# One-hots made earlier, a pair's gather moved between two parts of a down product, and other banks for the further rows' sums, in the expert layer of a two-layer encoder trunk

## The chip, the core and the metric

The kernel is one program on one core of a Trainium2 chip. The metric is the time of the whole program on the device in microseconds (us). The engines are named as the profile names them: PE is the matmul engine (PEld its weight loads), DVE the vector engine, ACT the scalar engine, POOL and SP the two others; SP issues nearly all loads. A PSUM bank is one of eight 128 x 512 float32 buffers into which PE writes.

## The reference, cut to what matters

256 rows of 1024 columns pass an even layer (mixers and a dense SwiGLU), an odd layer's banded attention, and then the expert layer, where the change is:

```python
def moe_swiglu(h, w_router, we_gate, we_up, we_down):
    t = h.reshape(b * s, d)                       # 256 x 1024
    logits = (t @ w_router).astype(F32)
    top_val, top_idx = lax.top_k(logits, TOP_K)   # 2 of 8 experts for each row
    gates = jax.nn.softmax(top_val, axis=-1)
    combine = jnp.einsum('tk,tke->te', gates, jax.nn.one_hot(top_idx, N_EXPERTS, dtype=F32))
    y = jnp.zeros_like(t)
    for e in range(N_EXPERTS):
        y = y + combine[:, e:e + 1] * ((silu(t @ we_gate[e]) * (t @ we_up[e])) @ we_down[e])
    return y
...
x = x + moe_swiglu(rms_norm(x, od_ffn_norm), ...)
```

The three weight tables of an expert are 1024 x 3584, 1024 x 3584 and 3584 x 1024 in float32: 352 MB for eight experts, read once.

## The kernel before

The expert layer begins at about 465 us of the span and lasts to its end. An expert computes only the rows that chose it. Their places (`pos`) are counted once; up to 64 of them are its *main* rows, up to 32 more its *further* rows ("over" in the code). A **one-hot** tile (`hot`, `hots`, through `one_hot` in line 910, on DVE) has a 1 where a row of the 256 goes to a place. The **gather** multiplies x with the one-hots on PE, so that an expert's rows stand turned in a tile `xg` (for even experts it lies in a tile that the trace calls oTh, for odd ones in xg); the products land in banks and DVE copies them out (line 935). One gather serves the two experts of a pair (2 and 3, 4 and 5, 6 and 7); experts 0 and 1 have one each.

The 3584 inner columns of an expert are cut into chunks of 512 to 2048 columns, and the loop at the end of `experts` goes over 18 chunks in a written order, the two experts of a pair one after the other by chunks, with the odd one's last chunk behind the even one's. For chunk i it runs the gate product (`cols`, ACT's Silu behind it), the up product (`cols`, DVE multiplies behind it), and then the down product of the chunk *before*, `down(i - 1, i)`. Each product comes in parts of up to four loaded weight tiles: main products of a part, then, under `arm`, the further rows' products of the same tiles. `arm` is a branch that every engine takes or passes by itself, on whether the expert has more than 64 rows. In this data the trace has products of the further rows for experts 1, 3, 5 and 7 and none for 0, 2, 4 and 6.

The down sums of an expert stand in two banks of its own for all its chunks: `y` (za in the trace) for the main rows, `yo` (zb) for the further ones. Behind an expert's last down part, its sums go back to the 256 rows: `split` (and `split_over` for the further rows) copies the bank as two float32r parts, ACT the high one and DVE the rest; products with the turned one-hot (`main_sums`, `over_sums`) bring them to row order, and DVE adds them, times the gate, to the total `yx` (`add_to`, line 1065). `turn` makes the turned one-hot dT of an expert when its last up product is done: one-hot on DVE, four products with an identity on PE, a copy on ACT. `turn_over` does this for the further rows one chunk later.

All other products (gate, up, transposes, gather, sums) write four banks in a fixed rotation: `banks(n)` hands out the next n and moves on, `banks(n, False)` only looks. They are named mm and tr in the trace.

What sets the order: within the expert layer PE, ACT and DVE each run their instructions in the order in which the code issues them (`in_order`). Loads go to SP's queue in the code's order (`feed.more` asks for as many tiles as were taken); a load waits there until its tile is free, that is, until PE has read what was in it.

Of the kernel before, what the change touches and what calls it, by code (L numbers as in the profile page):

```python
# [22 lines left out]
T = S // P  # L23
KB = D // P
# [23 lines left out]
def kernel(ctx: ExitStack, tc: tile.TileContext, A: dict, out: bass.AP):  # L48
# [9 lines left out]
    def mm(o, lhsT, rhs, start, stop):  # L58
        nc.tensor.matmul(o, lhsT, rhs, start=start, stop=stop, skip_group_check=True)  # L59
# [151 lines left out]
    x = consts.tile([P, T, D], F32, name="x")  # L211
# [610 lines left out]
    def starts(i):  # L822

        q = chunks[i + 1] if i + 1 < len(chunks) else None
        if not q or q.i or (q.e % 2 and q.e > 1):
            return []
        return [q.e] if q.e == 1 else [q.e, q.e + 1]
# [54 lines left out]
    with ExitStack() as ph:  # L882
# [31 lines left out]
        def hot(e):  # L914
            return one_hot(act.tile([P, T, CAP], F32, name="disp"), e, sel)

        def hots(es):

            o = act.tile([P, T, 2, CAP], F32, name="dispx")
            for j, e in enumerate(es):  # L920
                one_hot(o[:, :, j], e, selx)
            return o

        def gather(es, dx, kbs):

            m = len(es)
            nb = 4 // m
            for k in range(kbs[0], kbs[-1] + 1, nb):
                o = banks(1)[0][:, 0:4 * P].rearrange("p (b s) -> p b s", b=nb)
                for b in range(nb):  # L930
                    for t in range(T):
                        mm(o[:, b, 0:m * CAP].rearrange("p (e s) -> p e s", e=m), x[:, t, (k + b) * P:(k + b + 1) * P],
                           dx[:, t, 0:m], t == 0, t == T - 1)
                for j, e in enumerate(es):
                    nc.vector.tensor_tensor(rooms[e % 2][:, k:k + nb], o[:, :, j * CAP:(j + 1) * CAP],
                                            cst[:, C_GF1 + k:C_GF1 + k + nb, None].to_broadcast([P, nb, CAP]), op=OP.mult)
# [97 lines left out]
        class Expert:  # L1034
# [11 lines left out]

            def turn(self):
                self.dT = total[2][:, self.e % 2]
                self.dt = self.dt or hot(self.e)
                pt = banks(1)[0][:, 0:T * P].rearrange("p (t s) -> p t s", t=T)  # L1050
                self.turned(pt, MAIN, slice(0, MAIN))
                nc.scalar.activation(self.dT, pt, AF.Copy)
# [42 lines left out]

            def add_over(self, yy):
                self.split_over(yy)
                os = [banks(2) for _ in range(T)]
                self.over_sums(os, yy, True)
                for t in range(T):  # L1100
                    for h in range(2):
                        self.add_to(t, h, os[t][h])
# [41 lines left out]
        def banks(n, use=True):  # L1144
            found = [spin[(at[0] + i) % len(spin)] for i in range(n)]
            at[0] += n * use
            return found
# [9 lines left out]
        def experts(dt, feed, first, rvs):  # L1157


            found = [Expert(e, rvs[e] if rvs else None) for e in range(NE)]  # L1160
            found[0].dt, late = dt, []
            ao, turned, ready = aos, [], []

            def turn_main(i):
                n = chunks[i].n // 2
                turn(turned.pop()[:, 0:n], n, aTs[0][i % 2])

            def turn_over(i):
                n = chunks[i].n
                (turn_128 if by_128(n) else turn)(ao, over_width(n), aTs[1][i % 2])  # L1170

            def down(i, turns=None):
                q = chunks[i]
                x, cuts = found[q.e], spans(q.n // 256)
                for p, (i0, m) in enumerate(cuts):
                    dn = feed.take(m)
                    final = q.last and p == len(cuts) - 1
                    main_down(x.y, aTs[0][i % 2], i0, dn, q.n, q.i == 0, q.last)

                    def over():  # L1180
                        over_down(x.yo, aTs[1][i % 2], i0, dn, q.n, q.i == 0, q.last)

                    if turns and not p:
                        turn_main(turns)
                    if final and i == len(chunks) - 1:
                        x.finish(over)
                        return
                    if final:
                        x.split()
                        yy = act.tile([P, 2, 512], F32R, name="a")[:, :, 0:256]  # L1190
                    same = turns and not p and chunks[turns].e == q.e
                    with arm(x.rv):
                        over()
                        if same:
                            turn_over(turns)
                        if final:
                            x.add_over(yy)
                    if turns and not p and not same:
                        with arm(found[chunks[turns].e].rv):
                            turn_over(turns)  # L1200
                    feed.more(m)
                if q.last:
                    ready.append(x)

            def cols(x, main, over, n, mid=None, end=None):

                cuts = spans(KB // max(1, 2048 // n))
                nk = max(1, 2048 // n)
                for p, (i0, m) in enumerate(cuts):
                    tiles = feed.take(m)  # L1210
                    main_cols(main, x.xg, tiles, n, i0 * nk)
                    if mid and not p:
                        mid[0]()
                        with arm(mid[1]):
                            mid[2]()
                    if p == len(cuts) - 1:
                        end[0]()
                    with arm(x.rv):
                        over_cols(over, x.xg, tiles, n, i0 * nk)
                        if p == len(cuts) - 1:  # L1220
                            end[1]()
                    feed.more(m)

            for i, q in enumerate(chunks):
                x, n = found[q.e], q.n
                done = first and not i
                before = ready.pop() if ready else None
                m = len(parts(n))
                ow = over_width(n)
                part = ao[:, 0:ow]  # L1230

                def gate():
                    turned.insert(0, act.tile([P, 1024], F32, name="a"))
                    activate(turned[0], g, n)

                if done:
                    turned.append(act.tile([P, 1024], F32, name="a"))
                else:
                    g = banks(m)
                    go = banks(1)[0]  # L1240
                    mid = (lambda: turn_main(0), found[0].rv, lambda: turn_over(0)) if i == 1 else None
                    cols(x, g, go, n, mid, (gate, lambda: nc.scalar.activation(part, go[:, 0:ow], AF.Silu)))
                if late:
                    late.pop().turn_over()
                if before:
                    before.add(0)
                es = starts(i)
                if es:
                    dx = hots(es)

                def up():
                    a = turned[0]
                    if done:
                        g = banks(1)
                        first(g[0], 0)
                        nc.scalar.activation(a[:, 0:n // 2], g[0][:, 0:n // 2], AF.Copy)
                    activate(a, u, n, True)

                def up_over():
                    if done:  # L1260
                        go = banks(1)[0]
                        first(go, 1)
                        nc.scalar.activation(part, go[:, 0:ow], AF.Copy)
                    nc.vector.tensor_tensor(part, uo[:, 0:ow], part, op=OP.mult)

                u = banks(m)
                uo = banks(1)[0]
                cols(x, u, uo, n, None, (up, up_over))
                if es:
                    gather(es, dx, range(KB))  # L1270
                if before:
                    before.add(1)
                if q.last:
                    if not total:
                        total.extend(sums())
                    x.turn()
                    late.append(x)
                if i:
                    down(i - 1, i)
            late.pop().turn_over()  # L1280
            down(len(chunks) - 1)

# [107 lines left out]
        dx = hots([0])  # L1390
# [102 lines left out]
```

## Time and profile before

| | |
|---|---|
| time, median of 3 runs | 1319.26 us (1319.10 to 1319.53) |
| the profiled execution | 1318.28 us, of which its span is 1316.4 us |
| PE busy | 1269.1 us, 96% of the span |
| DVE busy, ACT busy | 380.1 us (29%), 322.0 us (24%) |
| PE's granted clock | 0.998 of full speed |
| bytes from HBM | 423.89 MB |

The span runs from the first to the last instruction; the profiled execution lies 1.9 us above its span and 1.0 us below the median. A view of instructions in order of time gives start, duration, engine, line, operation, out<-in by the program's names, the shape, the count, and in brackets how long the engine stood idle before and what released it. Idle times under 0.15 us are not shown in brackets. "PEq L1133" or "DVEq L1133" is the branch of `arm` as PE's or DVE's sequencer executes it. A product in float32 leaves two records (a transpose one), so counts in the trace are twice those of the program's order.

### The profile page before, as it was taken

The numbers are of one execution on the slowest core, as the hardware profiler recorded it, in microseconds if no ns is written. First come the engines' busy times: TensorE is split into PE (matmuls) and PEld (weight loads), VectorE is DVE, ScalarE is ACT, GpSimd is POOL, SyncE is SP. The second block draws the span as 40 slices with busy tenths as digits, with TensorE's granted clock in tenths as the row PEclk, the third lists the DMA queues.
The fourth block names the chain that finished last, engine by engine and source line by source line (L and its number), as shares of the span: only waits on it lengthen the run. The fifth ranks groups of instructions, "written<-read, shape, count | busy, mean of one in ns | idle before, by whom it ended". The sixth has DMA issues, their size and how long they took to land. (4 is left out here: it accounts for less than half of the span.)

```text
span 1316.4 us, 19363 instructions
## 1 busy us (share of the span) xinstructions
PE 1269.1 (96%) x7791; PEld 695.5 (53%) x7791; DVE 380.1 (29%) x735; ACT 322.0 (24%) x593; POOL 11.1 (1%) x38
## 2 busy tenths in 40 slices
PE   9999999999999989999999999999999999999996
PEld 6777888888777744343444333444333344333443
DVE  7965554446788510000111000111100001110001
ACT  7665544446566400100000000000000000000000
POOL 0000000000000000000000000000000000000000
PEclk9999999999999999999999999999999999999999
DMA  9623555555454989999899999999999999999980
GB/s 348 234 68 127 190 172 181 192 192 182 162 156 147 397 313 410 421 422 420 327 420 422 420 422 424 399 411 419 424 421 421 422 388 420 423 422 421 417 350 36
DMA packets 90245, 426.60 MB, mean 324 GB/s; under 512 B 7568, under 2 KB 10256, under 8 KB 59408
## 3 DMA queue, kind: packets, MB, share of 16 engines
q1 hardware_dynamic: 88768, 422.28, 80.4%
q0 software_dynamic: 640, 2.10, 0.7%
q8 instruction: 82, 1.34, 0.4%
q10 hardware_dynamic: 720, 0.60, 0.1%
q14 instruction: 35, 0.29, 0.1%
HBM read 423.89 MB, written 1.05 MB: 323 GB/s over the span
## 5 line engine op out<-in xcount | busy, mean ns | idle before, releaser
L59 PE MATMUL mm<-w,hTh 128*128 128x512 f32 x736 | 240.1, 400 | 0.9 <-DVE w L143 0.6
L143 DVE TENSOR_TENSOR w<-raw,w 128x1024 fp32r<-128x1024 f32 (+1 forms) x127 | 153.7, 1213 | 90.7 <-ACT w L142 90.2
L59 PEld LDWEIGHTS mm<-w,hTh 128*128 128x128 f32 x736 | 137.8, 188 | 33.3 <-DVE w L143 1.5
L142 ACT ACTIVATE w<-raw 128x1024 fp32r<-128x1024 f32 (+1 forms) x127 | 133.5, 1052 | 86.5 <-PE mm L59 51.3
L59 PE MATMUL mm<-w,hTl 128*128 128x512 f32 x368 | 146.5, 398 | 0.0
L1153 DVE TENSOR_TENSOR a<-tr,a 128x512 f32<-128x512 f32 (+1 forms) x16 | 10.0, 625 | 258.0 <-PE tr L59 151.9
L59 PE MATMUL za<-raw,hTh 128*64 128x512 f32 x360 | 81.5, 595 | 0.5 <-PEq L1133 0.4
L59 PEld LDWEIGHTS mm<-w,hTl 128*128 128x128 f32 x368 | 69.4, 188 | 14.8
L1153 DVE TENSOR_TENSOR a<-mm,a 128x512 f32<-128x512 f32 (+1 forms) x16 | 10.0, 624 | 222.7 <-PE mm L59 141.6
L59 PE MATMUL tr<-raw,xg 128*64 128x512 f32 (+4 forms) x400 | 63.8, 541 | 1.0 <-issue 0.4
L59 PE MATMUL tr<-rawb,xg 128*64 128x512 f32 (+4 forms) x504 | 59.6, 456 | 1.8 <-DVEq L1133 1.5
L59 PE MATMUL za<-rawb,hTh 128*64 128x512 f32 x256 | 57.6, 593 | 0.4 <-PEq L1133 0.4
L59 PE MATMUL mm<-w,oTh 128*64 128x512 f32 (+2 forms) x212 | 54.8, 517 | 2.4 <-DVEq L1133 1.5
L59 PE MATMUL mm<-raw,oTh 128*64 128x512 f32 (+1 forms) x232 | 47.2, 532 | 4.9 <-DVEq L1133 2.5
L59 PE MATMUL za<-w,hTh 128*64 128x512 f32 x224 | 50.5, 595 | 0.4 <-PEq L1133 0.4
L59 PEld LDWEIGHTS za<-raw,hTh 128*64 128x64 f32 x360 | 26.3, 137 | 46.0 <-issue 43.4
L59 PE MATMUL tr<-w,xg 128*64 128x512 f32 (+4 forms) x304 | 48.4, 530 | 0.3 <-PEq L1133 0.3
L59 PE MATMUL mm<-raw,xg 128*64 128x512 f32 (+4 forms) x320 | 48.3, 539 | 0.3 <-DMA rawb<-in_od_we_down 0.3
L255 DVE TENSOR_TENSOR oTl<-za,oTl 128x512 fp32r<-128x512 f32 x8 | 5.5, 690 | 138.5 <-ACT oTl L254 70.9
L59 PE MATMUL mm<-rawb,oTh 128*64 128x512 f32 (+1 forms) x204 | 42.9, 557 | 1.8 <-ACTq L1133 1.2
L981 ACT ACTIVATE hTh<-mm 128x512 f32<-128x512 f32 (+1 forms) x17 | 8.6, 544 | 141.3 <-PE mm L980 123.1
L59 PEld LDWEIGHTS tr<-rawb,xg 128*32 128x32 f32 (+1 forms) x504 | 24.0, 122 | 35.1 <-issue 29.2
(340 smaller groups left out, 1488.6 us busy)
## 6 DMA issues: line engine op xcount, KB each, us to landing
raw<-in_od_we_down SPq DMA_DIRECT2D x45, 1024.0 KB, 16.5
rawb<-in_od_we_down SPq DMA_DIRECT2D x32, 1024.0 KB, 18.4
raw<-in_od_we_gate SPq DMA_DIRECT2D x29, 1024.0 KB, 16.6
raw<-in_od_we_up SPq DMA_DIRECT2D x28, 1024.0 KB, 18.9
w<-in_od_we_down SPq DMA_DIRECT2D x28, 1024.0 KB, 16.8
rawb<-in_od_we_up SPq DMA_DIRECT2D x27, 1024.0 KB, 19.4
rawb<-in_od_we_gate SPq DMA_DIRECT2D x23, 1024.0 KB, 17.7
w<-in_od_we_gate SPq DMA_DIRECT2D x20, 1024.0 KB, 15.5
```

Source lines behind the costliest of these rows:

```text
L59: nc.tensor.matmul(o, lhsT, rhs, start=start, stop=stop, skip_group_check=True)
L142: nc.scalar.activation(hi[:, s], r[:, s], AF.Copy)
L143: nc.vector.tensor_tensor(lo[:, s], r[:, s], hi[:, s].bitcast(F32), op=OP.subtract)
L255: nc.vector.tensor_tensor(lo, src, hi.bitcast(F32), op=OP.subtract)
L981: nc.scalar.activation(dst[:, b:b + n], pt[:, 0:n], AF.Copy)
L1153: nc.vector.tensor_tensor(a[:, c:c + w], o[:, 0:w], a[:, c:c + w], op=OP.mult)
```

## The change

Three edits, and nothing else in the program:

1. The one-hot that `turn` needs is made for every expert's last chunk right behind the gate product (and the addition of t = 0 of an expert just finished), ahead of the up product, instead of in `turn`, behind the up product.
2. The gather for a new expert or pair is no longer issued behind the up product of chunk i and ahead of `turn`; it is handed to `down(i - 1, i, rows)` and issued behind that product's first part, with its transposes and further rows.
3. `add_over`, the further rows' sums, no longer takes four banks of the rotation. The sums of rows 0 to 127 (t = 0) go to the expert's own down banks `y` and `yo`; those of rows 128 to 255 go to the third and the fourth of the next four banks, without moving the rotation.

```diff
             def turn(self):
                 self.dT = total[2][:, self.e % 2]
-                self.dt = self.dt or hot(self.e)
...
             def add_over(self, yy):
                 self.split_over(yy)
-                os = [banks(2) for _ in range(T)]
+                os = [[self.y, self.yo], banks(4, False)[2:]]
                 self.over_sums(os, yy, True)
...
-            def down(i, turns=None):
+            def down(i, turns=None, rows=None):
...
                     feed.more(m)
+                    if rows and not p:
+                        gather(*rows, range(KB))
...
+                if q.last and not x.dt:
+                    x.dt = hot(q.e)
                 es = starts(i)
-                if es:
-                    dx = hots(es)
+                rows = (es, hots(es)) if es else None
...
                 cols(x, u, uo, n, None, (up, up_over))
-                if es:
-                    gather(es, dx, range(KB))
...
-                    down(i - 1, i)
+                    down(i - 1, i, rows)
```

**PE, around the first pair's gather**, behind the up product of expert 1's last chunk (in the names, dispx is the pair's one-hot and x the rows; disp is the one-hot of `turn`; za<-raw,hTh and za<-w,hTh are the first down part of expert 0; a and aos are what is transposed). Before:

```order
L59 MATMUL mm<-raw,xg 32x512 x8
L1133 UNCONDITIONAL_BRANCH x2
L59 MATMUL mm<-dispx,x 128x192 x4
L59 MATMUL tr<-dispx,x 128x192 x8
L59 MATMUL mm<-dispx,x 128x192 x4
L59 MATMUL mm<-ident,disp 64x128 x4
L59 MATMUL za<-raw,hTh 64x512 x8
L59 MATMUL za<-w,hTh 64x512 x8
```

After, from the first product behind the same branch:

```order
L59 MATMUL mm<-ident,disp 64x128 x4
L59 MATMUL za<-raw,hTh 64x512 x8
L59 MATMUL za<-w,hTh 64x512 x8
L980 MATMUL tr<-ident,a 128x128 x8
L1132 COMPARE_AND_BRANCH
L59 MATMUL zb<-raw,oTh 32x256 x16
L59 MATMUL zb<-w,oTh 32x256 x16
L1132 UNCONDITIONAL_BRANCH x2
L1132 COMPARE_AND_BRANCH
L980 MATMUL mm<-ident,aos 128x128 x4
L1132 UNCONDITIONAL_BRANCH x2
L59 MATMUL mm<-dispx,x 128x192 x4
```

The turned one-hot and the first down part now stand ahead of the gather, and the gather stands behind the transposes of expert 1's last chunk.

**DVE, at the same place** (line 910 is the one-hot, line 935 the gather's copies, L1153 and L1264 the multiplications behind the up product). Before:

```order
L1133 COMPARE_AND_BRANCH
L1264 TENSOR_TENSOR aos<-mm,aos 128x512
L1133 UNCONDITIONAL_BRANCH x2
L935 TENSOR_TENSOR oTh<-mm,cst 128x192
L935 TENSOR_TENSOR xg<-mm,cst 128x192
L935 TENSOR_TENSOR oTh<-tr,cst 128x192
L935 TENSOR_TENSOR xg<-tr,cst 128x192
L935 TENSOR_TENSOR oTh<-tr,cst 128x192
L935 TENSOR_TENSOR xg<-tr,cst 128x192
L935 TENSOR_TENSOR oTh<-mm,cst 128x192
L935 TENSOR_TENSOR xg<-mm,cst 128x192
L910 TENSOR_SCALAR disp<-slots,pos,sel 128x96 x2
```

After:

```order
L910 TENSOR_SCALAR disp<-slots,pos,sel 128x96 x2
L910 TENSOR_SCALAR dispx<-slots,pos,selx 128x96 x4
L1132 COMPARE_AND_BRANCH
L1132 UNCONDITIONAL_BRANCH x2
L1152 TENSOR_TENSOR a<-tr,a 128x512 x2
```

The one-hot of `turn` stood behind the gather's eight copies and now stands ahead of the multiplications behind the up product.

**DVE, at the end of expert 0's down product** (bank numbers kept; L255 are the parts of `split` and `split_over`, L1065 is `add_to`; the gate product that follows on PE begins in bank mm_3961, in both versions). Before:

```order
L255 TENSOR_TENSOR oTl_4778<-za_3962,oTl_4778 128x512
L1133 COMPARE_AND_BRANCH
L255 TENSOR_TENSOR a_5196<-zb_3964,a_5196 128x256
L1065 SCALAR_TENSOR_TENSOR yx_4775<-mm_3961,comb_3640,yx_4775 128x512
L1065 SCALAR_TENSOR_TENSOR yx_4775<-tr_3910,comb_3640,yx_4775 128x512
L1065 SCALAR_TENSOR_TENSOR yx_4775<-tr_3911,comb_3640,yx_4775 128x512
L1065 SCALAR_TENSOR_TENSOR yx_4775<-mm_3960,comb_3640,yx_4775 128x512
L1133 UNCONDITIONAL_BRANCH x2
```

After:

```order
L255 TENSOR_TENSOR oTl_4778<-za_3962,oTl_4778 128x512
L1132 COMPARE_AND_BRANCH
L255 TENSOR_TENSOR a_5196<-zb_3964,a_5196 128x256
L1064 SCALAR_TENSOR_TENSOR yx_4775<-za_3962,comb_3640,yx_4775 128x512
L1064 SCALAR_TENSOR_TENSOR yx_4775<-zb_3964,comb_3640,yx_4775 128x512
L1064 SCALAR_TENSOR_TENSOR yx_4775<-tr_3911,comb_3640,yx_4775 128x512
L1064 SCALAR_TENSOR_TENSOR yx_4775<-mm_3960,comb_3640,yx_4775 128x512
L1132 UNCONDITIONAL_BRANCH x2
```

Banks mm_3961 and tr_3910, in which the next gate product begins, are no longer read inside the branch.

## Rows read from the trace of the kernel before

**Rows 1.** Busy time by stretch: engines, PE's clock, DMA's share, GB/s

```profile
core 0: us, PE busy (x) PEld busy (x) DVE busy (x) ACT busy (x) POOL busy (x), PEclk, DMA share, GB/s
700.00:780.00 80.00, 76.86 (x488) 30.93 (x488) 9.80 (x19) 5.22 (x12) 0.00 (x0) 1.00 1.01 423
1280.00:1300.00 20.00, 18.26 (x218) 9.49 (x218) 4.01 (x8) 0.77 (x2) 0.00 (x0) 1.00 0.01 3
```

**Rows 2.** PE's waits: for whom, us in total, times, longest

```profile
PE tr L59 <- DVE disp L910: 5.5, 4, 1.7
PE mm L59 <- DVEq L1133: 4.0, 3, 1.5
PE mm L59 <- DVE disp L910: 3.3, 3, 1.4
PE tr L59 <- DVEq L1133: 3.0, 2, 1.5
...
PE mm L59 <- DMA rawb<-in_od_we_down: 0.7, 2, 0.4
```

**Rows 3.** Loads into tiles w, issued from 1176 to 1179 us

```profile
L838 SPq DMA_DIRECT2D w<-in_od_we_up x3: 327/328/423, 1176.7 to 1177.7; - x3
...
DMA to landing us min/median/max: 13.2/15.1/17.3
```

**Rows 4.** PE in order of time: the product that reads these tiles

```profile
1203.42 3.65 PE L59 MATMUL mm<-w,oTh 128*64 128x512 f32 x16
```

**Rows 5.** PE in order of time: products with one-hots of experts 0, 1, 2, 7

```profile
562.14 3.63 PE L59 MATMUL mm<-rawb,oTh 128*64 128x512 f32 x16
565.92 0.66 PE L59 MATMUL tr<-ident,disp 128*64 128x128 f32 x8
...
626.58 1.57 PE L59 MATMUL mm<-dispx,x 128*128 128x192 f32 x8
...
632.99 0.68 PE L59 MATMUL mm<-ident,disp 128*64 128x128 f32 x8 [0.95 <-DVE disp L910]
...
778.02 0.66 PE L59 MATMUL mm<-ident,disp 128*64 128x128 f32 x8 [1.43 <-DVE disp L910]
...
1287.88 0.68 PE L59 MATMUL tr<-ident,disp 128*64 128x128 f32 x8 [1.74 <-DVE disp L910]
```

**Rows 6.** PE in order of time: gate products behind a passed branch

```profile
470.73 0.65 PE L59 MATMUL mm<-raw,oTh 128*64 128x512 f32 x2 [0.93 <-DVEq L1133]
...
651.29 1.08 PE L59 MATMUL mm<-raw,oTh 128*64 128x512 f32 x4 [1.52 <-DVEq L1133]
...
747.55 0.65 PE L59 MATMUL tr<-rawb,oTh 128*64 128x512 f32 x2 [0.30 <-PEq L1133]
```

**Rows 7.** ACT and DVE in order of time, 649 to 652 us

```profile
649.81 0.60 ACT L254 ACTIVATE oTl<-za 128x512 fp32r<-128x512 f32 x1 [6.38 <-PE za L59]
...
650.44 0.69 DVE L255 TENSOR_TENSOR oTl<-za,oTl 128x512 fp32r<-128x512 f32 x1 [17.26 <-ACTq L1133]
```

**Rows 8.** All engines in order of time: expert 1's further sums

```profile
698.53 0.42 DVE L255 TENSOR_TENSOR a<-zb,a 128x256 fp32r<-128x256 f32 x1 [2.72 <-ACT a L254]
...
698.55 1.08 PE L59 MATMUL mm<-a,oTl 64*128 64x256 f32 x8 [0.50 <-ACT a L254]
...
699.67 1.41 DVE L1065 SCALAR_TENSOR_TENSOR yx<-mm,comb,yx 128x512 f32<-128x512 f32 x2 [0.71 <-PE mm L59]
...
700.52 2.80 PE L59 MATMUL mm<-rawb,xg 128*64 128x512 f32 x12 [0.41 <-issue]
```

**Rows 9.** PE in order of time: the gather's new place, 640 to 644 us

```profile
642.01 0.74 PE L980 MATMUL mm<-ident,aos 128*128 128x128 f32 x4 [0.31 <-PEq L1133]
642.68 1.51 PE L59 MATMUL za<-w,hTh 128*64 128x512 f32 x6
```

**Rows 10.** PE in order of time: start of expert 1's first gate product

```profile
495.03 1.08 PE L59 MATMUL tr<-raw,xg 128*64 128x512 f32 x4 [0.30 <-PEq L1133]
```

**Rows 11.** SP's loads in order of time, 624 to 650 us

```profile
626.71 15.91 SPq L838 DMA_DIRECT2D raw<-in_od_we_up  x4
642.71 7.51 SPq L838 DMA_DIRECT2D w<-in_od_we_up  x3
```

## The prediction

> **What bounds the kernel now.** I read first the busy time by stretch. In the expert layer two resources look full at once: from 700 to 780 us PE is busy for 76.86 of 80 us, and the DMA engines have a share of 1.01 at 423 GB/s [rows 1]. A full resource is not yet the one that sets the time, so the second view is that of PE's waits, which says for whom it stood still. For loads it hardly ever did: the largest such entry is 0.7 us in 2 waits. For DVE it stood still 5.5 + 4.0 + 3.3 + 3.0 = 15.8 us in 12 waits [rows 2]. The third look is at how early loads come. Three loads issued from 1176.7 to 1177.7 us land within 17.3 us at most, by 1195.0 us [rows 3]; they are the second to the fourth tile of the part whose product begins at 1203.42, so the last of them is first read three quarters into that row, 2.6 us later [rows 4]: a lead of 11.0 us. And from 1280 to 1300 us the DMA share is 0.01 while PE is busy for 18.26 us [rows 1]: everything has landed and PE still works. So PE's order of work sets the time, the loads keep a lead of some 11 us, and an idle stretch of PE in the expert layer counts in full. PE's clock is 1.00 in both stretches [rows 1], the full 2.4 GHz level, and no term below is one of the clock.
>
> **The change, part by part.** The reader should see in each case what PE waits for and what it would wait for next.
>
> *One-hots earlier.* Before, the one-hot of `turn` stands on DVE behind the multiplications of the up product, so PE has nothing to do between its last up product and the turned one-hot. Rows 2 have seven such waits, 5.5 + 3.3 = 8.8 us in all, and rows 5 one of each kind: 0.95 us for an odd expert behind the gather (three times, experts 1, 3, 5), 1.43 us for an even one (2, 4, 6), 1.74 us for expert 7, whose one-hot also stands behind two additions. Expert 0 shows what is left when the one-hot is there: its up product starts at 562.14 and takes 3.63, to 565.77, and the next product starts at 565.92, 0.15 us later [rows 5]; that is the passed branch. I charge this 0.15 us to the three even experts; the odd ones pass no idle branch there. Gain: 8.8 - 3 x 0.15 = 8.4 us. The instructions added are none, only moved. What hides the moved one-hot is the whole up product; queued behind it on DVE are the pair's one-hots, where there are any, and multiplications that wait for PE's up product. It may itself wait for PE to be past the earlier expert's `turn_over`, since both use one tile, but PE does that ahead of the same up product. Bounds: 7.9 us, if the branch costs 0.30 as in rows 6 at 747.55, and 8.6 us, if joints close up by some 0.06 us, as 642.68 lies ahead of the end of the row above it (642.75) [rows 9].
>
> *The gather moved.* Its 32 records run from 626.58 to 632.04 (632.99 less the idle 0.95) [rows 5], 5.46 us, three times for a pair, and shorter once for expert 1. They are the same products, with no wait named ahead of them, so a gain of their own is excluded. What the gather used to cover is the multiplication ahead of the first transposes; now the first down part covers it. The new risk is the banks: at the new place the rotation hands it banks that ACT has just copied transposes from, and the gather of expert 1 now stands directly ahead of the gate product that reads it [rows 10]. The nearest prices are a wait of 0.50 us for an ACT copy [rows 8], three times, and 0.95 us for DVE's last piece of work behind a gather [rows 5], once: 0 to 2.5 us lost. I take 0: the bank of the last transposes is the gather's fourth, three quarters of 5.46 us after its start, and the gate product's first part needs only the first of two DVE copies, made while the second half of the gather runs. SP's queue keeps its order; the four tiles of the first down part come free ahead of the gather, those of the second behind it.
>
> *Further sums in other banks, branch passed.* An even expert skips `add_over`, but the next gate product writes banks that DVE reads inside that branch, so PE waits until DVE has passed it; and DVE comes there only behind `split`: ACT 649.81 to 650.41, DVE 650.44 to 651.13 [rows 7], PE at 651.29 with 1.52 us idle [rows 6]. Rows 2 have 4.0 + 3.0 = 7.0 us in five such waits. One of them, 0.93 us at 470.73 [rows 6], belongs to another branch and stays; 6.1 us in four (experts 0, 2, 4, 6) are left. Afterwards the gate's two banks are last read by the gather's copies, long done. Next late is PE's own passing of the branch, 0.30 us, as at 747.55 [rows 6]. Gain: 6.1 - 4 x 0.3 = 4.9 us. Bounds: 4.9, and 6.1 - 4 x 0.93 = 2.4 us if each still waits as the product at 470.73 does.
>
> *The same, branch taken.* Experts 1, 3 and 5: the gate waits 0.41 us at 700.52 [rows 8] because DVE's first addition must empty its bank. That goes: 3 x 0.41 = 1.2 us. Against it, the second sum now lands in `yo`, which DVE still reads for 0.42 us at 698.53; but the result of that same DVE instruction is what PE's third product of this group waits for before the change, too. Bounds 1.2 - 3 x 0.42, about 0, and 1.4 with closed joints; I take 1.2. The Trainium skill's page "Perfetto Trace Analysis", section "Optimizing Tensor Performance" (Matmuls), advises independent matmul groups to rotate through different banks, so that one's evacuation overlaps the next; a sum put back into the bank being evacuated goes against it, and by that advice this term would be about 0 and the time 1306.0 us.
>
> Sum: 8.4 + 0 + 4.9 + 1.2 = 14.5 us. Against the profiled execution (1318.28 us, 1316.4 of span and 1.9 around it) this gives 1303.8; that execution lies 1.0 us below the median, and against the median 1319.26 the forecast is **1304.8 us**. Highest sum: 8.6 + 4.9 + 1.4 = 14.9, and idle times under 0.15 us, which the view does not name, could add at most 0.15 at each of the 14 places, 2.1: 17.0, or 1302.3. Lowest: 7.9 - 2.5 + 2.4 + 0 = 7.8, or 1311.5, if everything goes badly at once; I take half of that way, 1308.5, as the forecast's own upper end.
>
> **The rivals.**
>
> *The branch wait stays.* The gate product still waits for DVE by a running count, and if that count is one that DVE reaches only behind `split` or in the branch, edit 3 does nothing for the even experts. For it: the wait is on DVE both times. Against it: DVE's last read of these banks is now the gather's copy. It costs the 4.9 us: 1309.7 us. This is also the case in which the change does not do what it says.
>
> *The loads set the time.* For it: DMA share 1.01 over the stretch [rows 1]. Then idle PE time inside the layer only moves, and what is gained is what lies behind the last landing: expert 7's 1.74 us [rows 5], in a stretch without loads [rows 1]: 1317.5 us, no change that can be told. Against it: the waits of rows 2 and the lead of 11.0 us [rows 3, 4]. By then PE gains the 14.5 us less 1.7, 1.3 and 1.2 for the places of experts 7 and 6 that come later, 10.3 us: less than the lead, even if the loads, issued sooner, gain nothing. The Trainium skill's page "Perfetto Trace Analysis", section "Identifying the Most-Contended Engine", judges DMA by HBM utilization and TensorE not by matmul busy time, and its "HBM Reference", section "Specifications (TRN2)", gives about 425 GB/s for a core streaming alone. By that rule DMA is the engine to work on here and the time would be this rival's 1317.5; the trace agrees on the rate (423 GB/s) but not on who waits.
>
> *Slower, through SP's queue.* Loads pause while PE gathers: four loads went out in a stretch of 15.91 us from 626.71, and the next only at 642.71 [rows 11], for want of free tiles. If the gather between two down parts adds a second pause of its own 5.46 us at each of three pairs, 16.4 us, instead of moving the one there is, the loads fall behind; it decides from where the added pauses exceed the lead of 11.0 us. Price: 1317.5 + 16.4 - 11.0 = 1322.9 us. Against it: before, the pause spans gather and first down part together; now the first part's tiles come free ahead of the gather, so the one pause is cut in two.
>
> **How the numbers follow.** Forecast 0.84, branch wait stays 0.08, loads set the time 0.05, slower 0.03. The forecast's own range, 1302.3 to 1308.5, holds perhaps 0.9 of its 0.84; with the first rival's 1309.7 taken in, the range 1302.3 to 1310.0 holds 0.84, and the other two are left out. What a measurement of this kernel can tell from no change is about 0.2%, 2.6 us. Faster by more: 0.84 + 0.08 = 0.92. Within: 0.05. Slower: 0.03.
>
> **What would show it.** In the waits of PE, the seven waits for disp should be gone and the waits for DVE's branch should be one of 0.93 us. The turned one-hot should follow the up product within 0.15 us, the gather the transposes without a wait, and the gate behind an even expert should show 0.30 us for PE's own branch. If the gather shows waits for ACT, or expert 1's first gate product one for DVE, the second part was mis-sized; if waits for loads appear and grow through the layer, the second or third rival holds. The forecast is wrong from the ground up if PE's gaps are gone and the span is not shorter by their sum.

## The result and the profile after

The changed kernel takes **1304.71 us** (median of 4 runs, 1304.04 to 1306.10); the kernel before, in the same set, 1319.18 us (4 runs, 1318.50 to 1319.53). The ratio is 0.9892, 95% interval 0.9875 to 0.9909: 14.5 us faster. The profiled execution of after is the longest of the four: 1306.10 us, span 1303.9. It is used here for its gaps, not for its length: its expert layer, from the first product of the layer to the last, takes 828.0 us (466.57 to 1294.60) against 842.9 (465.26 to 1308.15) in the profiled execution of before. That is 14.9 us less. The spans differ by 12.5 us only, because this execution loses 2.4 us outside the layer: the layer begins 1.3 us later, and what follows its last product takes 1.1 us longer.

Busy time by stretch, the view of [rows 1]: the bounds of the stretch, its length, then busy time (and instructions) of PE, PEld, DVE, ACT and POOL, PE's clock, the DMA share and GB/s.

```profile
700.00:780.00 80.00, 78.48 (x496) 31.09 (x494) 7.70 (x14) 5.22 (x12) 0.00 (x0) 1.00 1.01 422
...
1279.00:1294.00 15.00, 15.00 (x170) 7.17 (x168) 1.11 (x2) 2.74 (x7) 0.00 (x0) 1.00 0.01 1
```

From 700 to 780 us PE is busy 78.48 us where it was 76.86 [rows 1]; the DMA engines stand where they stood, at 422 GB/s. The last 15 us are again without loads, and PE has no gap in them.

PE's waits of after, the view of [rows 2]: for whom, us in total, times, the longest. Line 1132 is the branch that was 1133.

```profile
PE tr L59 <- PEq L1132: 4.7, 17, 0.4
PE mm L59 <- PEq L1132: 3.6, 13, 0.4
...
PE mm L59 <- DVEq L1132: 0.9, 1, 0.9
PE mm L59 <- DMA rawb<-in_od_we_down: 0.6, 2, 0.3
```

The seven waits for disp are gone, and of the five for DVE's branch the one of 0.93 us is left. PE's own passing of branches is now the largest entry. Loads still hold PE up by nothing that counts.

PE in order of time around the first pair's gather (start, duration, engine, line, operation, out<-in, shape, count, and in brackets the idle time before it and its releaser), which answers to [rows 5, 6, 9]:

```profile
627.84 0.66 PE L59 MATMUL mm<-ident,disp 128*64 128x128 f32 x8
628.33 3.60 PE L59 MATMUL za<-raw,hTh 128*64 128x512 f32 x16
...
636.83 0.74 PE L980 MATMUL mm<-ident,aos 128*128 128x128 f32 x4 [0.31 <-PEq L1132]
637.41 1.47 PE L59 MATMUL mm<-dispx,x 128*128 128x192 f32 x8
638.71 2.76 PE L59 MATMUL tr<-dispx,x 128*128 128x192 f32 x16
641.31 1.46 PE L59 MATMUL mm<-dispx,x 128*128 128x192 f32 x8
642.71 5.37 PE L59 MATMUL za<-w,hTh 128*64 128x512 f32 x24
...
650.20 2.79 PE L59 MATMUL mm<-raw,oTh 128*64 128x512 f32 x12 [0.40 <-PEq L1132]
...
655.88 3.65 PE L59 MATMUL mm<-rawb,oTh 128*64 128x512 f32 x16 [0.30 <-PEq L1132]
...
661.58 0.65 PE L59 MATMUL mm<-ident,disp 128*32 128x128 f32 x16 [0.32 <-PEq L1132]
```

The turned one-hot (627.84) has no wait ahead of it any more. The gather starts at 637.41 directly behind the transposes of the further rows, at the place that the prediction gave, and none of its four banks waits for ACT. The gate product of the next expert (650.20) waits 0.40 us for PE's own branch in place of 1.52 us for DVE's.

Three further places of the same view: the one-hot of expert 2, the gate product behind expert 6, the one-hot of expert 7:

```profile
775.38 0.66 PE L59 MATMUL mm<-ident,disp 128*64 128x128 f32 x8 [0.30 <-PEq L1132]
...
1262.05 5.56 PE L59 MATMUL tr<-rawb,xg 128*64 128x256 f32 x96 [0.16 <-PEq L1132]
...
1274.36 0.66 PE L59 MATMUL tr<-ident,disp 128*64 128x128 f32 x8
```

And behind expert 1's last down part, where the branch is taken [rows 8]:

```profile
697.50 0.38 PE L59 MATMUL za<-a,oTl 64*128 64x256 f32 x1 [0.50 <-ACT a L254]
697.96 0.39 PE L59 MATMUL zb<-a,oTl 64*128 64x256 f32 x1
...
698.42 0.74 PE L59 MATMUL tr<-a,oTl 64*128 64x256 f32 x8
699.10 1.08 PE L59 MATMUL mm<-rawb,xg 128*64 128x512 f32 x4
```

The 0.50 us for ACT's copy is there as before; the 0.41 us ahead of the gate product is gone.

What became of the lead of the loads: the landing of one load that SP issued at 1182.2 us, and the row of PE that reads it, as the third of the three tiles that it spans.

```profile
L846 SPq DMA_DIRECT2D raw<-in_od_we_down x1: 328/328/328, 1182.2 to 1182.2; - x1
...
DMA to landing us min/median/max: 21.2/21.2/21.2
```

```profile
1203.71 5.35 PE L59 MATMUL za<-raw,hTh 128*64 128x512 f32 x24
```

It lands at 1203.4 and is first read two thirds into the row, at 1207.1: 3.8 us. By the same reading, tile by tile over all 358 loads of the layer, this is the smallest lead after; before, the smallest was 10.7 us. So most of the lead was spent, and without harm: the rate did not change, the loads come nearly when they came (the last one lands 2.7 us sooner), and PE comes 9 us sooner at chunk 15 (counted from 0) and 13.5 us at the end.

### The profile page after: what moved, and what is told of

It is laid out like the page before. It is cut to its first block, busy times and chain, and to the rows that moved or that the text cites. A ratio compares the mean times of both kernels' runs of the same rounds, so it can differ in the third digit from the quotient of the medians.

```text
span 1303.9 us, 19371 instructions
## 1 busy us (share of the span) xinstructions
PE 1270.2 (97%) x7791; PEld 697.0 (53%) x7791; DVE 379.8 (29%) x735; ACT 321.9 (25%) x593; POOL 11.0 (1%) x38
## 5 line engine op out<-in xcount | busy, mean ns | idle before, releaser
L59 PEld LDWEIGHTS mm<-w,hTh 128*128 128x128 f32 x736 | 138.5, 189 | 31.9 <-issue 1.3
L59 PEld LDWEIGHTS mm<-w,hTl 128*128 128x128 f32 x368 | 69.8, 190 | 14.9
L1154 ACT ACTIVATE a<-tr 128x512 f32<-128x512 f32 (+1 forms) x16 | 8.5, 530 | 136.8 <-PE tr L59 136.8
L59 PE MATMUL mm<-rawb,xg 128*64 128x512 f32 (+4 forms) x280 | 42.0, 541 | 0.0
## 6 DMA issues: line engine op xcount, KB each, us to landing
rawb<-in_od_we_gate SPq DMA_DIRECT2D x23, 1024.0 KB, 19.7
```

What stands on the lines that cost most here:

```text
L1154: nc.scalar.activation(a[:, c:c + w], o[:, 0:w], AF.Silu)
```

## The experiments

All kernels of a set ran on one chip beside the kernel before, which stood at 1318.6 us (first set, e1 to e4), 1318.78 (second, a0 to x9) and 1319.15 (third, x7 and x8).

**One-hots alone** (edit 1).

```diff
-                self.dt = self.dt or hot(self.e)
...
+                if q.last and not x.dt:
+                    x.dt = hot(q.e)
```

> The first edit alone: the one-hots are made ahead of the up product, the gather stays behind it, the sums keep their four banks. Theory (each edit removes its own waits of PE and nothing else): the seven waits for disp go, as they did in the changed kernel (0.95 to -0.07 three times, 1.43 to 0.32 three times, 1.74 to -0.07), 8.2 us: 1311.0 us, and the waits for DVE's branch stay at 1.5 us. Rival (an odd expert's one-hot only helps because the gather no longer stands ahead of it): three waits of 0.95 us stay, 1314.0 us.

Measured: 1310.51 us (1310.39 to 1310.81), ratio 0.9934 (0.9918 to 0.9951), 8.1 us less than before. PE's waits of this kernel:

```profile
PE mm L59 <- DVEq L1132: 4.0, 3, 1.5
...
PE tr L59 <- DVEq L1132: 3.0, 2, 1.5
```

The waits for the branch stand as in [rows 2], the waits for disp are gone from the list. The first term of the sum is real by itself.

**Banks alone** (edit 3).

```diff
-                os = [banks(2) for _ in range(T)]
+                os = [[self.y, self.yo], banks(4, False)[2:]]
```

> The third edit alone: other banks for the further rows' sums, the rest as before. Theory: the four waits for DVE's branch fall from 1.5 to about 0.3 us and the three of 0.41 us go, less 0.45 for the second gate parts that then show PE's own branch: 5.9 us, 1313.3 us. Rival (the gain of these banks needs the gather's copies as the last readers, so it comes only with the moved gather): only the 1.4 us of the taken branches, 1317.8 us.

Measured: 1312.62 us (1312.02 to 1314.77), ratio 0.9954 (0.9937 to 0.9971), 6.0 us less. Here it is the other way round; the waits for disp stand as they stood:

```profile
PE tr L59 <- DVE disp L910: 5.5, 4, 1.7
...
PE mm L59 <- DVE disp L910: 3.3, 3, 1.4
```

**Both, with the gather in its old place** (edits 1 and 3: both diffs above).

> The first and the third edit, the gather left where it was. Theory (PE's order sets the time and the moved gather is worth nothing by itself): within 0.6 us of the changed kernel, 1304.7 us. Rival (the moved gather pays through the loads, whose pause it shortens, or costs through its banks): more than 1 us away from it, 1306.3 us if loads become late, with waits for loads in PE's list.

Measured: 1304.68 us (1304.56 to 1305.47), ratio 0.9891 (0.9875 to 0.9908). That is the changed kernel's time, and 13.9 us less than before, where the two edits alone add up to 14.1. Its layer takes 828.5 us in the profile, and the changed kernel's 828.0 in both of its profiles, so the moved gather is worth some 0.5 us there, too little for the times to tell. Around the gather PE has no wait in the old place either, once the one-hot comes earlier:

```profile
630.78 1.46 PE L59 MATMUL mm<-dispx,x 128*128 128x192 f32 x8
632.17 0.66 PE L59 MATMUL mm<-ident,disp 128*64 128x128 f32 x8
```

**Gather and banks, one-hots late** (edits 2 and 3: the diff of the change without its first edit).

> The second and the third edit, the one-hots left in turn. Theory: the third edit's 5.9 us come, the waits of the even experts and of expert 7 stay, and the odd experts' waits grow from 0.95 to about 1.43 us, since without the gather only the multiplications and the one-hot lie between the up product and the turned one-hot, and PE has nothing to do meanwhile: a gain of 5.9 - 3 x 0.48 + 0.3 = 4.8 us, 1314.4 us. Rival (the moved gather takes the odd experts' waits away by itself): 5.9 + 3.1 = 9.0 us, 1310.2 us.

Measured: 1313.34 us (1312.60 to 1315.36), ratio 0.9953 (0.9937 to 0.9970): 0.7 us above the banks alone, within their spread. PE now waits 1.20 us for an odd expert's one-hot in place of 0.95 [rows 5], since the gather no longer stands between; the second row is expert 7's:

```profile
628.84 0.66 PE L59 MATMUL mm<-ident,disp 128*64 128x128 f32 x8 [1.20 <-DVE disp L910]
...
1282.95 0.82 PE L59 MATMUL tr<-ident,disp 128*64 128x128 f32 x8 [1.85 <-DVE disp L910]
```

So moving the gather gains nothing that the times show in either company, and without the earlier one-hots it uncovers 3 x 0.25 us. Expected were 0.48 us at each, up to the 1.43 us of an even expert; the wait stopped short of that.

**The same banks, the wrong two** (the change, one index altered).

```diff
-                os = [[self.y, self.yo], banks(4, False)[2:]]
+                os = [[self.y, self.yo], banks(4, False)[:2]]
```

> The changed kernel once more, beside the three others of this set, so that differences of 1 to 4 us can be read against it. Every theory: 1304.7 us, as its first runs.

> The changed kernel with one number moved: the further rows' second pair of sums takes the first two of the next four banks, which the gate product behind the branch writes, in place of the last two. Theory (a bank that VectorE reads inside the branch keeps the product that writes it next waiting until VectorE has passed the branch, whether the branch is taken or not): the four waits behind passed branches come back (4 x 1.5 less 4 x 0.32, about 4.7 us) and the three taken branches now wait for VectorE's additions (1.3 to 1.8 us each, about 5 us), so 1314.5 us, between 1312 and 1317. Rival (what the change gains there comes from two sums at a time in place of one, whichever banks they are in): 1304.7 us.

Measured: the changed kernel 1304.07 us (1303.63 to 1304.53), this one 1316.00 us (11 runs, 1314.44 to 1317.32), ratio to the kernel before 0.9978 (0.9969 to 0.9987). PE's waits:

```profile
PE mm L59 <- DVEq L1132: 3.9, 3, 1.5
...
PE mm L59 <- issue: 3.2, 2, 1.6
PE tr L59 <- DVEq L1132: 3.0, 2, 1.5
...
PE tr L59 <- issue: 1.6, 1, 1.6
```

The waits for DVE's branch are back with their old totals, and each of the three taken branches costs 1.6 us (the view puts them down to issue, as it did the 0.41 us of [rows 8]). The whole layer of each kernel in the view of busy time, this one first (length of the stretch, then PE's busy time):

```profile
465.52:1304.78 839.26, 812.03 (x5562) 338.47 (x5562) 76.75 (x151) 59.79 (x122) 0.00 (x0) 1.00 0.96 397
```

```profile
465.95:1293.94 827.99, 810.16 (x5562) 336.62 (x5562) 76.80 (x151) 59.79 (x122) 0.00 (x0) 1.00 0.97 403
```

The layer is 11.3 us longer: PE is idle 9.4 us longer and busy 1.9 us longer, 1.3 of these at a lower clock (last section). So two sums at a time are not what helps; what counts is that no bank that DVE reads inside the branch is one that the gate product writes next. A passed branch kept such a bank for 1.5 us, about as long as a taken one (1.6 us): PE waited until DVE was past it.

**Half of the gather left out** (the change, with the gather over rows 0 to 127 alone; the other 128 rows' part of the sum is not computed).

```diff
-                    for t in range(T):
+                    for t in range(1):
                         mm(o[:, b, 0:m * CAP].rearrange("p (e s) -> p e s", e=m), x[:, t, (k + b) * P:(k + b + 1) * P],
-                           dx[:, t, 0:m], t == 0, t == T - 1)
+                           dx[:, t, 0:m], True, True)
```

> The changed kernel, where the gather products run over the first 128 of the 256 token rows alone, which leaves out the other half of that sum: 3 x 5.46/2 + 2 x 3.7/2 = about 11.9 us less TensorE work in the expert layer, no load left out. Theory A (TensorE sets the end throughout, the loads' smallest lead of 3.8 us is enough): 1292.8 us. Theory B (a load lands only so much earlier as its buffer comes free, and not at all once SP's queue runs without a pause, so the lead of 3.8 us is used up and the rest of the gain goes into waits for loads): 1298 to 1301 us, with TensorE waits of some 5 to 8 us for weight loads that the changed kernel doesn't have.

Measured: 1294.06 us (1293.00 to 1295.12), 10.0 us below the changed kernel. In the layer the three pair gathers fell from 5.37 to 2.77 us and expert 1's from 3.78 to 2.00, 9.6 us in all; the layer became 8.6 us shorter. The missing 1.0 us is found in one part, the second half of the up product of chunk 15, which takes 8.22 us where it took 7.09. PE in order of time, and the waits for loads behind 1100 us that the changed kernel doesn't have:

```profile
1181.50 3.05 PE L59 MATMUL mm<-w,oTh 128*64 128x512 f32 x12
1185.21 1.08 PE L59 MATMUL mm<-w,oTh 128*64 128x512 f32 x4 [0.66 <-DMA w<-in_od_we_up]
```

```profile
PE mm L59 <- DMA w<-in_od_we_up: 0.7, 1, 0.7
...
PE mm L59 <- DMA raw<-in_od_we_up: 0.3, 1, 0.3
```

Neither theory had it quite. The time is near that of A, 1.3 us above it, because the loads too came some 7 us sooner at that place (SP could issue them sooner as tiles came free); but the lead there has gone from 4.6 us to zero. PE sets the end of the changed kernel, with some 9 us of room before loads begin to cost.

**Two banks skipped, and further rows first** (a version meant to beat both; then each half alone). Skipped banks, at the gate and ahead of the up product of chunk 1:

```diff
+                if i == 1:
+                    banks(2)
```

Further rows first: in an expert's last down part, if that isn't its first part too, the further rows' products and `split_over` run under a branch of their own, ahead of the main rows' products:

```diff
+                    early = final and p
+                    if early and i < len(chunks) - 1:
+                        yy = act.tile([P, 2, 512], F32R, name="a")[:, :, 0:256]
+                        with arm(x.rv):
+                            over()
+                            x.split_over(yy)
                     main_down(x.y, aTs[0][i % 2], i0, dn, q.n, q.i == 0, q.last)
...
-                        over()
+                        if not early:
+                            over()
```

and `add_over` uses `yo` and the last three of the next four banks.

> A version meant to be faster than both: the changed kernel with two banks skipped ahead of the gate and of the up product of chunk 1 (they wait 0.93 us for VectorE and 1.19 us for ScalarE to pass a branch), and in the last down part the further rows issued ahead of the main rows, so that their branch no longer stands between the main products and the gate. Theory: less the two waits (1.7 us) and part of the passed branches' 0.3 to 0.5 us each (about 1.8 us): 1301.2 us. Rival (the branches cost the same wherever they stand, and the shrunken lead of the loads takes the rest): 1303 us or above.

> The changed kernel with only the two skipped banks ahead of the gate and of the up product of chunk 1. Theory: its two waits on VectorE's and ScalarE's passing of a branch (0.93 and 1.19 us) go down to TensorE's own passing, about 0.3 us each, so 1.5 us less than the changed kernel's 1304.1: 1302.6 us, all of what the joint version gained. Rival (the loads' lead of 3.7 us is what the gain goes into): 1304 us.

> The changed kernel with only the last down part's further rows issued ahead of its main rows. Theory, after the joint version gained 1.5 and not 2.9 us: TensorE pays its own passing of a branch (0.3 to 0.6 us) wherever the branch stands, so this half gives 1304 us, within 0.4 us. Rival (it gains 1.8 us and the skipped banks gain nothing): 1302.3 us.

Measured: both 1302.58 us (1301.86 to 1303.60, ratio 0.9880, 0.9865 to 0.9895); skipped banks alone 1302.75 us (1302.07 to 1304.22, ratio 0.9874, 0.9857 to 0.9890); further rows first alone 1304.03 us (1303.14 to 1305.53, ratio 0.9878, 0.9862 to 0.9894). The intervals of the three ratios overlap with that of the changed kernel (0.9873 to 0.9903), so by their times none of them is shown to be faster. PE with the banks skipped, at the two places where the changed kernel waits 0.93 and 1.19 us:

```profile
470.53 1.94 PE L59 MATMUL tr<-raw,oTh 128*64 128x512 f32 x8 [0.47 <-ACTq L1132]
...
478.77 1.51 PE L59 MATMUL mm<-rawb,oTh 128*64 128x512 f32 x6 [0.72 <-PEq L1132]
```

Of 2.1 us, 1.2 are left; 0.3 us at each had been expected, so the residue was undersized. The layers say more than the times. By the view used for the wrong two banks, from first to last product, with skipped banks, with further rows first, and with both:

```profile
465.52:1292.32 826.80, 810.01 (x5562) 335.65 (x5562) 76.75 (x151) 59.79 (x122) 0.00 (x0) 1.00 0.98 403
```

```profile
466.58:1292.72 826.14, 809.03 (x5562) 336.43 (x5562) 76.60 (x151) 59.79 (x122) 0.00 (x0) 1.00 0.98 404
```

```profile
465.30:1290.54 825.24, 808.90 (x5562) 337.74 (x5562) 76.50 (x151) 59.75 (x122) 0.00 (x0) 1.00 0.98 404
```

The changed kernel's layer takes 827.99 us in one profile and 828.03 in the other. So, in one profiled execution each, the skipped banks are worth 1.2 us of the layer, the further rows first 1.9, and both together 2.8, near the 2.9 first expected. What follows the last product, the same program in all of them, takes 8.0 us with skipped banks and 10.8 with further rows first (8.2 and 9.3 in the two profiles of the changed kernel), and such differences hide the second half's gain in four times. The expectation that this half gives nothing had been read off the time of the joint version, and it is not borne out by the layers. The list of waits doesn't show this gain either: here PE waits 1.4 us in all for its own branch ahead of the further rows, where the changed kernel has 1.5 us for ACT's copy ahead of the sums:

```profile
PE zb L59 <- PEq L1132: 1.4, 3, 0.5
```

A part of it lies behind these waits: at expert 1 the gate product starts 1.15 us behind the first sum (698.19 and 697.04), where in the changed kernel it takes 1.60 (699.10 and 697.50 above).

## Why the prediction was right

The forecast was 1304.8 us and the time 1304.71. That PE's order of work sets the time, and that each removed wait counts in full, is what the runs bear out; that the total agrees to 0.1 us is luck, since the four runs spread over 2.1 us and small misses cancel below. The terms, with the idle times that the trace of after has at the same places:

- **One-hots earlier, forecast 8.4 us (7.9 to 8.6): 8.2 us.** The odd experts' 3 x 0.95 us and expert 7's 1.74 us went wholly, and their joints closed by 0.07 us more. The even ones kept 0.30 to 0.35 us each, not the 0.15 us taken from expert 0 [rows 5]: the other end named, the 0.30 us of [rows 6], was right. The edit alone gave 8.1 us (the layer: 8.2).
- **The gather moved, forecast 0 (0 to 2.5 lost): about 0, some 0.5 us gained by the layers.** No product of the gather waits for ACT's copies, and expert 1's first gate product directly behind its gather has no wait, where it had 0.30 us for PE's branch [rows 10]. That branch went elsewhere: PE now waits 0.16 us ahead of the down part and 0.15 ahead of the gather, where it waited 0.16 ahead of the gather and 0.30 behind it.

The two rows of after for that, the gather and the gate product behind it:

```profile
492.48 3.78 PE L59 MATMUL mm<-dispx,x 128*128 128x96 f32 x32 [0.15 <-PEq L1132]
496.19 1.08 PE L59 MATMUL tr<-raw,xg 128*64 128x512 f32 x4
```

- **Branch passed, forecast 4.9 us (2.4 to 4.9): 4.9 us**, from waits of 0.40, 0.31, 0.31 and 0.16 us in place of 6.1 us.
- **Branch taken, forecast 1.2 us (0 to 1.4): 1.1 us.** The three waits of 0.41 us went. From the first sum to the gate product it is now 1.60 us (697.50 to 699.10) where it was 1.97 [rows 8], 0.37 us less, and the same within 0.01 us at the two other experts. `yo` was not quite free: before, the first two products of the sums started together (698.55, in the first of the two rows), and now the second, the first one into `yo` (697.96), starts 0.46 us behind, when DVE has read the bank. That makes the sums 0.1 us longer each time. The reason given holds for the third product, which waits for this read anyway, and the second was overlooked. Here the Trainium skill's page "Perfetto Trace Analysis", section "Optimizing Tensor Performance" (Matmuls), with its rotation through different banks, would have expected none of this gain; the measurement speaks against it at this place, as the bank put to use again is emptied by an instruction on which the products behind depend in any case.
- **Not foreseen, and nearly cancelling:** behind experts 0, 2 and 4, the second part of the gate product now waits 0.30 us for PE's branch (655.88 above) where it had 0.15 us: 0.45 us lost. `turn_over` of experts 1, 3 and 5 (661.58) waits 0.32 us in place of 0.43: 0.3 us gained. With the gather in its old place (e3) the two waits are 0.15 and 0.43 us, so both come with the moved gather. Why PE takes a branch in 0.15 us at one place and in 0.3 or 0.4 at another no run here settles.

These terms give some 14.1 us (8.2 + 4.9 + 1.1 - 0.45 + 0.3). By the view of busy time PE's idle time in the layer fell by 14.1 us (from 31.9 to 17.8) and its busy time by 0.7; the layer became 14.9 us shorter. One sum of the prediction was off without effect: half of the way from 1304.8 to 1311.5 is 1308.1, not 1308.5.

**The rivals.** *The branch wait stays* (1309.7): the gate product's wait for DVE is gone in e2 and in the changed kernel, and the experiment with the wrong two banks shows what it costs if it isn't. *The loads set the time* (1317.5): this rival fell, since the gaps that went did not come back as waits for loads. The counterargument, 10.3 us of gain against a lead of 11.0, held, but the room it left was small: at the place where the lead was read it fell from 11.0 to 4.6 us, and elsewhere to 3.8. Leaving out half of the gather was enough for the first waits. The rule of the Trainium skill's "Perfetto Trace Analysis" ("Identifying the Most-Contended Engine") picked another engine than the one that paid here: the DMA engines ran at 423 GB/s before and 422 after, and the removed waits of PE still counted in full. *Slower, through SP's queue* (1322.9): SP's loads in order of time, as [rows 11]:

```profile
627.97 9.48 SPq L838 DMA_DIRECT2D raw<-in_od_we_up  x4
637.54 12.71 SPq L838 DMA_DIRECT2D w<-in_od_we_up  x3
```

The first row has shrunk from 15.91 to 9.48 us, and the second has grown from 7.51 to 12.71. The longest pause between two loads in each was 14.3 and 6.5 us before, and it is 7.9 and 11.8 us now: the queue paused twice before, too, and the gather's time went from the first pause to the second. In sum they are 1.2 us shorter (19.7 us, where it was 20.9). So the prediction was right that no pause is added, though it counted one pause before where there were two.

## What to carry to other kernels

A bank that is used only inside a skipped branch can still hold up whoever writes it next: here PE waited 1.5 us until DVE had passed the branch, and the wait went when such work got banks that the product behind the branch doesn't write. When two resources both look full, look for the lead of the loads (landing to first read) at its smallest place: while it was above zero here, a shorter order of work paid in full. It is a cautious measure of what is left, since loads come sooner too when their tiles come free sooner: at 3.8 us of lead, 9.6 us less work still gave 8.6. And take what is left of a removed wait from several places of the same kind, not from the smallest example.

## What the runs showed of the hardware

PE's clock can fall in a short wait. In the kernel with the wrong two banks one of the three waits of 1.62 us is followed by a stretch at half clock, and where the one-hots came late the wait of 1.85 us is. Busy time by stretch, columns as above, the clock being the third number from the right; PE's last product before this ends at 909.8, and the next begins at 911.43:

```profile
909.00:910.00 1.00, 0.81 (x13) 0.60 (x11) 0.74 (x2) 0.00 (x0) 0.00 (x0) 1.00 1.06 418
910.00:911.00 1.00, 0.00 (x0) 0.00 (x0) 1.00 (x3) 0.00 (x0) 0.00 (x0) 0.87 0.99 406
911.00:912.00 1.00, 0.57 (x2) 0.33 (x4) 0.99 (x2) 0.00 (x0) 0.00 (x0) 0.50 1.01 412
...
914.00:915.00 1.00, 1.00 (x8) 0.44 (x6) 0.00 (x0) 0.00 (x0) 0.00 (x0) 0.93 1.00 418
```

From within the idle time to some 914 us the granted clock is 0.50, the 1.2 GHz level. From the start of the product behind the wait (911.43) to that of a later one (916.23) it takes 4.80 us, and 3.49 us in the changed kernel (906.54 to 910.03): 1.3 us, beside the wait. In the kernel with late one-hots the clock is 0.50 from 1284 to 1286 us. More such falls would explain why the 11 runs of the kernel with the wrong two banks spread over 2.9 us, though only one of them has a profile to show it: the shortest, 1314.44, has a mean clock of 0.998, the longest two, 1317.32, 0.995. The same spread is in the kernel before (15 runs, 0.998 and 1317.77 at the short end, 0.996 to 0.997 and 1321.2 at the long one), which has waits of 1.5 to 1.7 us; the four runs of the changed kernel beside it, with no such wait in the layer, keep 0.998 to 0.999 and lie within 0.9 us. The mean clock alone is no proof: the changed kernel's run of 1306.10 us has 0.997, and its profile shows the granted clock fall to 0.50 only behind the last product. So a wait of this length cost, in two profiled executions, more than itself. Why one of three equal waits is followed by it and the others are not stays open here.

A load that is issued sooner landed sooner by less in this layer, where the DMA engines are busy throughout (share 1.01): the last of the three loads of [rows 3] was issued at 1177.7 us and took 17.3 us to land; after, the same load was issued at 1172.2 and took 19.9 us. Issued 5.5 us sooner, it landed 2.8 us sooner.
